# A short bfloat16 product of constants behind 38 columns of a two-block transformer kernel

## The chip, the core and the metric

The kernel runs on one core of a Trainium2 chip. The metric is the device time of one execution, in microseconds (us). The core's engines are TensorE (PE in the profile; its weight loads are listed as PEld), VectorE (DVE), ScalarE (ACT), GpSimd (POOL) and SyncE (SP). Each takes its instructions in order from a queue of its own, and they wait for one another by semaphores. The granted clock is the share of TensorE's full clock that the profile records.

## What is computed

A sequence of 256 tokens of width 1024 goes through two blocks in float32. The first has latent attention, retention, cross attention to a memory and a mixture of experts. The second is the part where the change lies:

```python
def hybrid_layer(x, p_i, ...):
    h = rmsnorm(x, g_mix)
    z = h @ w_in                       # seven parts of 1024 columns
    ...
    y_rnn = jax.nn.gelu(rnn_y) * rg_lru(rnn_x, ...)
    merged = jax.nn.sigmoid(gate_rnn) * y_rnn + jax.nn.sigmoid(gate_conv) * y_conv
    x = x + merged @ w_out
    h = rmsnorm(x, g_ffn)
    g, u = jnp.split(h @ w_gate_up, 2, axis=-1)
    x = x + (jax.nn.silu(g) * u) @ w_down
    gate = jax.nn.sigmoid(rmsnorm(x, g_ple) @ w_ple_gate)
    x = x + gate * (p_i @ w_ple)
```

The output is the root-mean-square norm of the result.

## The kernel before

Activations are kept transposed: features on the 128 partitions, the 256 tokens along the free dimension, so a vector of 1024 features is eight tiles of 128x256. A **column** is one such tile of the result of a dense layer. It is made by `dense_w` (lines 237 to 244): for each tile of 128 input features it takes a 128x128 block of weights and issues three products of 256 columns into one PSUM tile `d`. Three are needed because both sides are split into a high and a low part in a type that TensorE takes in one pass (float32r): high by high, low by high, high by low. A column of an input of 1024 features is 24 products, a column of the down projection (2816 features) 66.

The weights come from memory in chunks on SyncE's queue (line 175, tiles `w`, `r` and others). `Stream.split` makes units of 128x512 of them: ScalarE copies the unit into its high part `wh` (line 199), VectorE subtracts to get the low part `wl` (line 200). `Stream.blk` keeps up to three units split ahead. PSUM tiles `d` come from the pool `psd` with four buffers; the pool `psa` has three buffers of one bank each, for tiles called `a`.

The parts around the change, in the order of the program:

- Four heads of gates and recurrences. The recurrence of the second pair of heads is put off in small pieces (`bg`, run by `tick`), which are exponentials, squares, a root and scans on ScalarE and VectorE.
- Lines 1234 to 1238: eight columns `ps = col()` of 24 products; each is read by a gelu on ScalarE (line 1238, tile `xc`), which is ordered behind the root of the recurrences. The products of the gates before these columns read tile `xch`.
- Eight columns of gates, then the output projection with its residual, each with evictions on both engines; the second begins with a lead group of two columns (`lead`, line 253).
- Lines 1268 to 1277: 22 pairs of columns, gate and up, of 24 products each. VectorE scales the gate column (1272), ScalarE takes the silu, VectorE scales again (1274) and multiplies with the up column `pu` (1276); the result is split into `ach` and `acl`.
- Lines 1287 to 1292: eight columns of the down projection; VectorE adds the residual (1290) and both engines split the sum.
- Eight columns of the last gate and projection, and a tail with the final norm, whose statistic takes a tile `a` of `psa`.

Between the columns stand the sums of squares for the norms: four products each (line 332, tile `st`), one output column wide, with float32 operands. `keep_warm` (line 384) issues bfloat16 products of 256 columns of constants, 24 at the start and 16 in the first block.

The code is written with a framework that keeps the order of the program on each engine where nothing else decides, sets the semaphores itself, and reuses a pool's buffer once all that touched the tile before is done. `tc.issue_after(i)` orders the instructions in its block behind instruction `i` of the same engine.

Of the kernel before, what the change touches and what calls it, by code (L numbers as in the profile page):

```python
# [9 lines left out]
F32 = mybir.dt.float32  # L10
F32R = mybir.dt.float32r
I32 = mybir.dt.int32
BF16 = mybir.dt.bfloat16
# [5 lines left out]
P = 128  # L19
# [20 lines left out]
AHEAD = 3  # L40
LEAD_O = 3
LEAD_2 = 2

# [64 lines left out]
def block_kernel(tc, wst, cst_d, csa_d, sml_d, rw_d, dec_d, xt_d, pt_d, pos_d, out_d, dbg=None):  # L110
    nc = tc.nc
    V, S, TE = nc.vector, nc.scalar, nc.tensor
# [6 lines left out]
    psa = tc.alloc_tile_pool(name="psa", bufs=3, space=PSUM)  # L119
# [13 lines left out]
    cst = glob.tile([P, NCST], F32, name="cst")  # L133
# [7 lines left out]
    def G(name, i=0, n=1):  # L141
        a, _ = SML[name]
        return sml[:, a + i:a + i + n]
# [6 lines left out]
    class Stream:  # L150
# [28 lines left out]
        def split(self):  # L179

            if self.cpos >= CHUNKS[self.chunk]:
                nx = self.chunk + 1
                while nx in RAW:
                    nx += 1
                if nx >= self.limit:
                    return False
                self.tiles.pop(self.chunk, None)
                self.chunk = nx
                self.cpos = 0
            self.load(self.chunk + 1)  # L190
            w = self.tiles[self.chunk]
            n = min(UNIT, CHUNKS[self.chunk] - self.cpos)
            src = w[:, self.cpos:self.cpos + n]
            wh = self.wsp.tile([P, UNIT], F32R, name="wh")
            wl = self.wsp.tile([P, UNIT], F32R, name="wl")
            with contextlib.ExitStack() as st:
                for i in self.after:
                    st.enter_context(tc.issue_after(i.ins))
                S.activation(wh[:, :n], src, AF.Copy)  # L199
                V.tensor_sub(wl[:, :n], src, wh[:, :n].bitcast(F32))  # L200
            self.ready.append((wh, wl, n))
            self.cpos += n
            return True
# [26 lines left out]
    def split_g(h, l, x, g):  # L230
        S.mul(h, x, g)
        return V.scalar_tensor_tensor(l, x, g, h.bitcast(F32), op0=OP.mult, op1=OP.subtract)
# [5 lines left out]
    def dense_w(ps, kts, h, l):  # L238
        n, last = 0, 3 * len(kts) - 1
        for kt in kts:  # L240
            wh, wl = ws.blk(P)
            for a, b in ((wh, h), (wh, l), (wl, h)):
                TE.matmul(ps, a, b[:, kt], start=n == 0, stop=n == last)  # L243
                n += 1

    def lead(kts, h, l, n):

        pst = [ps_d() for _ in range(n)]
        for i, kt in enumerate(kts):
            for ps in pst:  # L250
                wh, wl = ws.blk(P)
                for j, (a, b) in enumerate(((wh, h), (wh, l), (wl, h))):
                    TE.matmul(ps, a, b[:, kt], start=i == 0 and j == 0, stop=i == len(kts) - 1 and j == 2)  # L253
        return pst

    def columns(n, kts, h, l, nl=0):
        pre = lead(kts, h, l, nl)
        for m in range(n):
            if m < nl:
                yield pre[m]  # L260
            else:
                ps = ps_d()
                dense_w(ps, kts, h, l)
                yield ps
# [9 lines left out]

    def ps_d():
        return psd.tile([P, T], F32, name="d")

    last_rsqrt = []
    last_sum = []
# [127 lines left out]
    for m in range(4):  # L407
        ps = ps_d()
        dense_w(ps, range(KT), xh, xl)
        if m < 3:  # L410
            split_g(ch[:, m], cl[:, m], ps, G("qn_g", m) if m < 2 else G("kvn_g"))
            S.activation(csq[:, m], ps, AF.Square)
            for tt in range(2):
                TE.matmul(cps[:, m // 2, tt:tt + 1], csq[:, m, tt * P:(tt + 1) * P], ones, start=m != 1 and tt == 0,
                          stop=m > 0, skip_group_check=True)
        else:
            S.mul(kpe, ps, G("kg_r"))
            S.activation(ksq[:, 4], ps, AF.Square)
        for kt in (2 * m, 2 * m + 1):
            sq.add(x0[:, kt])  # L420
# [10 lines left out]
    for m in range(6):  # L431
        ps = ps_d()
        dense_w(ps, range(2), ch, cl)
        S.activation(qsq[:, m], ps, AF.Square)
        for tt in range(2):
            TE.matmul(qst[:, 4 * tt:4 * tt + 4], qsq[:, m, tt * P:(tt + 1) * P], selh[:, m] if m < 4 else selr[:, m - 4],
                      start=m == 0 and tt == 0, stop=m == 5, skip_group_check=True)
        if m < 4:
            V.tensor_scalar(qn[:, m], ps, G("qg_n"), None, op0=OP.mult)
        else:  # L440
            S.mul(qr[:, m - 4], ps, G("qg_r"))
    kst = psa.tile([P, 2, 5], F32, name="a")
    for m in (4, 0, 1, 2, 3):
        if m < 4:
            ps = ps_d()
            dense_w(ps, (2,), ch, cl)
            S.activation(ksq[:, m], ps, AF.Square)
        for tt in range(2):
            TE.matmul(kst[:, tt, m:m + 1], ksq[:, m, tt * P:(tt + 1) * P], ones if m < 4 else C("selk")[:, 0:1],
                      start=True, stop=True)  # L450
# [155 lines left out]
    n = 0  # L606
    for h in range(4):
        if h >= 2:
            latent(h - 2)
        for m in (2 * h, 2 * h + 1, None):  # L610
            ps = ps_d()
# [57 lines left out]
    for m in range(KT):  # L669
        if m in (1, 4):  # L670
            latent(2 + m // 4)
        ps = next(cols)
# [60 lines left out]
    for h in range(4):  # L733
        ss = SumSq()
        cqT = ctmp.tile([P, 2, T], F32, name="cqT")
        for k2 in range(2):
            ps = next(cols)
# [7 lines left out]
        for it in range(2):  # L745
            sl = slice(it * P, (it + 1) * P)
            ps = psa.tile([P, T], F32, name="a")
# [15 lines left out]
    for m, ps in enumerate(columns(KT, range(KT), oh_, ol_, LEAD_O)):  # L763
# [7 lines left out]
        for tt in range(2):  # L771
            TE.matmul(lps[:, tt], xg[:, tt * P:(tt + 1) * P], rw[:, m], start=m == 0 and tt == 0,
                      stop=m == KT - 1, skip_group_check=True)
# [227 lines left out]
    for g in range(NGRP):  # L1001
# [12 lines left out]
        last = g == NGRP - 1  # L1014
# [22 lines left out]
        a = smp.tile([P, T], F32, name="ss_acc")  # L1037
# [54 lines left out]
    with tc.issue_after(mm.ins):  # L1092
        for m in range(3, KT):
            for tt in range(2):
                TE.matmul(sq3[:, tt:tt + 1], qs[:, m, tt * P:(tt + 1) * P], ones,  # L1095
                          start=m == 3 and tt == 0, stop=m == KT - 1, skip_group_check=True)
# [22 lines left out]
    def tick(n=1):  # L1119
        for _ in range(min(n, len(bg))):  # L1120
            bg.pop(0)()

    def col(raw=False):
        ps = ps_d()
        dense_w(ps, range(KT), *(rawx if raw else nrm))
        tick()
        return ps
# [55 lines left out]
    for h in range(4):  # L1183
# [33 lines left out]
        for dst, bias in ((ri, "br"), (ii, "bi")):  # L1217
            for m in range(2):
                ps = ps_d()
# [7 lines left out]
        if h == 0:  # L1227
            nrm = hl()
            for kt in range(KT):
                t = zt.tile([P, T], F32, name="t3")  # L1230
# [2 lines left out]
    show("xc", xc)  # L1233
    for m in range(KT):
        ps = col()
        tick(1 if m else 5)
        with tc.issue_after(roots[0].ins):
            S.activation(xc[:, m], ps, AF.Gelu_apprx_tanh)
# [13 lines left out]
    sq4 = SumSq()  # L1252
    for m, ps in enumerate(columns(KT, range(KT), mgh, mgl, LEAD_2)):
        V.tensor_add(x4[:, m], ps, x3[:, m])
# [14 lines left out]
    for f in range(FT):  # L1269
        pg = next(cols)  # L1270
        tg = ft.tile([P, T], F32, name="tg")
        V.tensor_mul(tg, pg, r4b)
        S.activation(tg, tg, AF.Silu)
        V.tensor_mul(tg, tg, r4b)
        pu = next(cols)
        V.tensor_mul(tg, pu, tg)
        split(ach[:, f], acl[:, f], tg)

# [8 lines left out]
    for m in range(KT):  # L1287
        ps = ps_d()
        dense_w(ps, range(FT), ach, acl)
        V.tensor_add(x5[:, m], ps, x4[:, m])  # L1290
        split_g(x5h[:, m], x5l[:, m], x5[:, m], G("ple_g", m))
        sq5.add(x5[:, m], last=m == KT - 1)
# [9 lines left out]
    for m in range(KT):  # L1302
        pl = ps_d()
        dense_w(pl, range(2), pth, ptl)
        ps = ps_d()
        dense_w(ps, range(KT), x5h, x5l)
        t = ft.tile([P, T], F32, name="tg")
# [19 lines left out]
    for m in range(KT):  # L1327
        V.tensor_mul(x6[:, m], x6[:, m], r6b)  # L1328
        if m % 2 == 0 or m == KT - 1:
            a = max(m - 1, 0) if m < KT - 1 else m  # L1330
# [49 lines left out]
def _blocks_w(w, cols, kts, lead=0):  # L1380

    k = w.shape[0]
    a = w.reshape(k // P, P, w.shape[1])
    parts = [a[t][:, c] for t in range(kts if lead else 0) for c in cols[:lead]]
    parts += [a[:, :, c].transpose(1, 0, 2).reshape(P, -1) for c in cols[lead:]]
    return np.concatenate(parts, 1)
# [7 lines left out]
def _cols(lo, n):  # L1394
    return [np.arange(lo + P * m, lo + P * (m + 1)) for m in range(n)]


def _pack(inp):
# [29 lines left out]
    def col(o, c):  # L1428
        return [np.arange(P) + P * c + D * o]
# [10 lines left out]
    for o in (1, 5):  # L1440
        parts.append(_blocks_w(w, [col(o, c)[0] for c in range(KT)], 8))
    parts.append(_blocks_w(g("w_out_2")[0], _cols(0, 8), 8, LEAD_2))
    w = g("w_gate_up_2")[0]
# [93 lines left out]
```

## Time and profile before

| | |
|---|---|
| median of 3 runs | 884.67 us |
| the runs | 881.99, 884.67, 886.38 us |
| the profiled execution | 884.14 us, of which the span is 882.5 us |
| mean granted TensorE clock | 0.983 |
| TensorE products, weight loads | 6508 each |
| dense products of `dense_w` over tiles `hh`, `ll` | 3624, 280 to 282 ns each |

A row of the profile gives the line of the kernel, the engine, the operation and the tiles, output before the arrow and inputs behind it, with the numbers of buffers left out. The products are pipelined: one has a duration of 280 ns, but the next starts about 117 ns after it. So a price of TensorE's time is read from the distance of the starts, not from durations. The span runs from the first to the last instruction; times of rows count from its start.

### The profile page before, as it was taken

To read this page: it belongs to the slowest core of one execution; us is meant where nothing else is said; L and a number is where in the kernel's file an instruction comes from. 1 tells how busy PE (TensorE), PEld (TensorE's weight loads), DVE (VectorE), ACT (ScalarE), POOL (GpSimd) and SP (SyncE) were. 2 spreads that over 40 slices of the span, in tenths; PEclk is the share of its full clock that TensorE was granted. 3 is DMA by queue.
4 is the path that set the end of the run, shared out by engine and by line. 5 is a ranking of instruction groups with operands and counts; after the bars stand their busy time and mean duration, and the time that the engine had idled before them with its cause. 6 is when DMAs were issued, how large, how long until landed. Compare 5 with 4: busy or idle time off the path is not lost.

```text
span 882.5 us, 16760 instructions
## 1 busy us (share of the span) xinstructions
PE 834.6 (95%) x6508; PEld 722.4 (82%) x6508; DVE 558.2 (63%) x1445; ACT 460.4 (52%) x947; POOL 3.0 (0%) x9
## 2 busy tenths in 40 slices
PE   8999999999899998699789999999999999999995
PEld 7888897999784554244349999999999999999995
DVE  6798868767663111011059959757987777766675
ACT  7696565665422111011046778777766555555563
POOL 0000000000000000000000000000000000000000
PEclk9999999999999999899989999999999999999998
DMA  8253543579769999999997546555655555553401
GB/s 326 97 209 143 192 155 113 184 296 402 302 266 410 425 426 422 423 424 423 427 423 274 202 154 215 192 179 202 208 187 192 184 179 181 182 186 136 135 16 48
DMA packets 32677, 214.90 MB, mean 244 GB/s; under 512 B 3792, under 2 KB 4688, under 8 KB 8272
## 3 DMA queue, kind: packets, MB, share of 16 engines
q1 hardware_dynamic: 31680, 212.06, 62.5%
q8 instruction: 53, 0.87, 0.4%
q0 software_dynamic: 336, 1.05, 0.3%
q10 hardware_dynamic: 576, 0.66, 0.2%
q14 instruction: 32, 0.26, 0.1%
HBM read 212.70 MB, written 1.05 MB: 242 GB/s over the span
## 4 chain that ended last, share of the span: by engine, by line
PE 49%; DMA 6%; DVE 2%; ACT 1%; issue 0%; DVEq 0%; ACTq 0%; SPq 0%
PE d L243 43%; DMA w<-wst 3%; DMA ll<-wst 2%; PE a L1021 2%; PE a L1072 1%; PE d L1058 1%; PE d L253 1%; PE st L855 1%; PE a L855 1%; ACT wh L199 0%; DVE xs L1328 0%; DVE wl L200 0%; ACT aa L1158 0%; PE a L1095 0%; DVE hs L1170 0%
## 5 line engine op out<-in xcount | busy, mean ns | idle before, releaser
L243 PE MATMUL d<-hh,wl 128*128 128x256 f32 x1208 | 340.2, 282 | 1.3 <-DVE wl L200 1.2
L243 PE MATMUL d<-hh,wh 128*128 128x256 f32 x1208 | 339.9, 282 | 1.1 <-ACT wh L199 1.1
L243 PE MATMUL d<-ll,wh 128*128 128x256 f32 x1208 | 338.4, 280 | 0.0
L199 ACT ACTIVATE wh<-w 128x512 fp32r<-128x512 f32 (+1 forms) x291 | 180.1, 627 | 135.6 <-PE d L243 103.6
L200 DVE TENSOR_TENSOR wl<-w,wh 128x512 fp32r<-128x512 f32 (+1 forms) x291 | 197.2, 685 | 60.8 <-ACT wh L199 57.7
L243 PEld LDWEIGHTS d<-hh,wl 128*128 128x128 f32 x1208 | 227.8, 189 | 2.8 <-DVE wl L200 2.3
L243 PEld LDWEIGHTS d<-ll,wh 128*128 128x128 f32 x1208 | 228.0, 189 | 1.2 <-issue 1.0
L243 PEld LDWEIGHTS d<-hh,wh 128*128 128x128 f32 x1208 | 226.9, 188 | 2.3 <-ACT wh L199 1.6
L199 ACT ACTIVATE wh<-r 128x512 fp32r<-128x512 f32 (+1 forms) x126 | 77.3, 623 | 53.4 <-PE d L243 48.8
L200 DVE TENSOR_TENSOR wl<-r,wh 128x512 fp32r<-128x512 f32 (+1 forms) x126 | 84.7, 681 | 29.0 <-ACT wh L199 27.1
L243 PE MATMUL d<-ach,wl 128*128 128x256 f32 x176 | 49.3, 280 | 0.0
L243 PE MATMUL d<-ach,wh 128*128 128x256 f32 x176 | 49.1, 279 | 0.0
L243 PE MATMUL d<-acl,wh 128*128 128x256 f32 x176 | 49.1, 279 | 0.0
L1081 DVE COPY y<-a 128x256 f32<-128x256 f32 x16 | 6.8, 424 | 60.6 <-ACT y L1080 60.6
L1038 ACT ACTIVATE ss_acc<-a,gsl 128x256 f32<-128x256 f32 x8 | 3.8, 474 | 75.6 <-DVE gsl L1028 54.2
L1058 PEld LDWEIGHTS d<-ss_sq,y 128*128 128x128 f32 x128 | 23.0, 190 | 14.9 <-ACT y L1080 6.6
L1058 PE MATMUL d<-ss_sq,y 128*128 128x256 f32 x128 | 31.6, 388 | 3.1 <-ACT y L1080 2.6
L243 PEld LDWEIGHTS d<-acl,wh 128*128 128x128 f32 x176 | 33.1, 188 | 0.0
L243 PEld LDWEIGHTS d<-ach,wl 128*128 128x128 f32 x176 | 33.0, 188 | 0.0
L243 PEld LDWEIGHTS d<-ach,wh 128*128 128x128 f32 x176 | 32.9, 187 | 0.0
L855 PEld LDWEIGHTS a<-ss_sq,xt 128*128 128x128 f32 x136 | 16.9, 191 | 15.4 <-issue 6.7
L855 PEld LDWEIGHTS st<-ss_sq,xt 128*128 128x128 f32 x120 | 14.9, 191 | 14.0 <-issue 7.5
(456 smaller groups left out, 1236.4 us busy)
## 6 DMA issues: line engine op xcount, KB each, us to landing
w<-wst SPq DMA_DIRECT2D x83, 1024.0 KB, 4.9
r<-wst SPq DMA_DIRECT2D x39, 1024.0 KB, 5.0
rx<-wst SPq DMA_DIRECT2D x28, 1024.0 KB, 17.4
ll<-wst SPq DMA_DIRECT2D x9, 1024.0 KB, 19.5
hh<-wst SPq DMA_DIRECT2D x9, 1024.0 KB, 19.5
rz<-wst SPq DMA_DIRECT2D x8, 1024.0 KB, 19.5
ck<-wst SPq DMA_DIRECT2D x5, 1024.0 KB, 19.6
cv<-wst SPq DMA_DIRECT2D x5, 1024.0 KB, 19.6
```

What stands on the lines that cost most here:

```text
L199: S.activation(wh[:, :n], src, AF.Copy)
L200: V.tensor_sub(wl[:, :n], src, wh[:, :n].bitcast(F32))
L243: TE.matmul(ps, a, b[:, kt], start=n == 0, stop=n == last)
L253: TE.matmul(ps, a, b[:, kt], start=i == 0 and j == 0, stop=i == len(kts) - 1 and j == 2)
L855: TE.matmul(ps[:, j], xt[:, tt, kt * P:(kt + 1) * P], oneh[:, tt], start=tt == 0, stop=tt == 1)
L1021: TE.matmul(pg[32 * q:32 * q + 32], xgs[:, kt, 32 * q:32 * q + 32], w[:, 512 * q:512 * q + 512], start=kt == 0, stop=kt == KT - 1)
L1038: S.activation(a, pg[:, 0:T], AF.Silu, scale=gsl[:, 4:5])
L1058: mm = ins = TE.matmul(acc[m], y[:, m % 4 * P:(m % 4 + 1) * P], sc, start=False, stop=last, skip_group_check=True)
L1072: ins = TE.matmul(py[32 * q:32 * q + 32], at[:, f, 32 * q:32 * q + 32], w[:, 512 * q:512 * q + 512], start=f == 0, stop=f == 1)
L1081: V.tensor_copy(y[:, 256:512], py[:, 256:512])
```

## The change

A function `beat(n)` is added. It issues one bfloat16 product: the first 128 columns of the constants' identity matrix, read as 256 bfloat16 values, give the 128x128 weights (the first 128) and the moving side (the first n), and the result goes into a tile `a` of `psa` that all beats share and nobody reads. `dense_w` records its last product, and the beat is ordered behind it. A beat is issued behind each of the eight gelu columns, behind each of the 22 up columns and behind each of the eight down columns, with n = 32, 64, 128, 256 by turns.

```diff
+BEATS = (32, 64, 128, 256)
...
         for kt in kts:
             wh, wl = ws.blk(P)
             for a, b in ((wh, h), (wh, l), (wl, h)):
-                TE.matmul(ps, a, b[:, kt], start=n == 0, stop=n == last)
+                last_product[:] = [TE.matmul(ps, a, b[:, kt], start=n == 0, stop=n == last)]
                 n += 1
...
+    last_product = []
+    beats = []
+
+    def beat(n):
+
+        t = cst[:, 0:128].bitcast(BF16)
+        if not beats:
+            beats.append(psa.tile([P, 512], F32, name="a"))
+        with tc.issue_after(last_product[0].ins):
+            TE.matmul(beats[0][:, 0:n], t[:, 0:P], t[:, 0:n], start=True, stop=True)
...
     for m in range(KT):
         ps = col()
+        beat(BEATS[m % 4])
         tick(1 if m else 5)
...
         pu = next(cols)
+        beat(BEATS[f % 4])
         V.tensor_mul(tg, pu, tg)
...
         dense_w(ps, range(FT), ach, acl)
+        beat(BEATS[m % 4])
         V.tensor_add(x5[:, m], ps, x4[:, m])
```

## Rows read from the trace of the kernel before

**Rows 1.** The page, first part: busy time and share of each engine.

```profile
PE 834.6 (95%) x6508; PEld 722.4 (82%) x6508; DVE 558.2 (63%) x1445; ACT 460.4 (52%) x947; POOL 3.0 (0%) x9
```

**Rows 2.** Stretches from 560 us on: length, busy (count) per engine, clock, DMA.

```profile
core 0: us, PE busy (x) PEld busy (x) DVE busy (x) ACT busy (x) POOL busy (x), PEclk, DMA share, GB/s
560.00:600.00 40.00, 39.44 (x335) 39.23 (x335) 28.14 (x55) 30.31 (x59) 0.00 (x0) 1.00 0.48 168
600.00:840.00 240.00, 239.82 (x2038) 239.65 (x2037) 179.94 (x351) 143.29 (x269) 0.54 (x1) 1.00 0.51 182
```

**Rows 3.** TensorE's waits from 580 us to 882 us.

```profile
PE a L332 <- DVE ss_sq L318: 2.0, 1, 2.0
PE st L354 <- DVE r L1325: 1.4, 1, 1.4
PE d L243 <- DVE wl L200: 0.6, 1, 0.6
PE st L354 <- DVE r L304: 0.2, 1, 0.2
```

**Rows 4.** The chain that ended last, dense phase: start, us, what.

```profile
599.17 32.55 PE d L243 x274
...
660.40 181.97 PE d L243 x1545
```

**Rows 5.** The same chain from 580 us to 600 us.

```profile
582.81 0.63 ACT wh L199
...
598.52 0.61 DVE wl L200
```

**Rows 6.** TensorE's products around 599 us, in order of time.

```profile
598.34 0.28 PE L243 MATMUL d<-ll,wh 128*128 128x256 f32 x1
599.17 0.39 PE L243 MATMUL d<-hh,wl 128*128 128x256 f32 x1 [0.56 <-DVE wl L200]
```

**Rows 7.** The chain again: last products into an `a` tile before.

```profile
462.46 0.34 PE a L1095 x4
```

**Rows 8.** Products and weight loads around a sum of squares at 654 us.

```profile
654.05 0.28 PE L243 MATMUL d<-hh,wl 128*128 128x256 f32 x1
654.17 0.50 PE L332 MATMUL st<-cst,ss_acc 128*128 128x1 f32 x4
...
654.73 0.28 PE L243 MATMUL d<-ll,wh 128*128 128x256 f32 x1
...
654.06 0.53 PEld L332 LDWEIGHTS st<-cst,ss_acc 128*128 128x128 f32 x4
654.50 0.19 PEld L243 LDWEIGHTS d<-hh,wh 128*128 128x128 f32 x1
```

**Rows 9.** Weight loads of bfloat16 products of 32 columns, first block.

```profile
262.68 0.12 PEld L826 LDWEIGHTS <-oneb 128*128 128x128 bf16 x2 [0.48 <-issue]
262.73 0.12 PEld L826 LDWEIGHTS <-ltb 128*128 128x128 bf16 x2
262.78 0.17 PEld L826 LDWEIGHTS <-oneb 128*128 128x128 bf16 x4
```

**Rows 10.** The 16 bfloat16 products of `keep_warm` and the one ahead.

```profile
260.13 0.38 PE L789 MATMUL d<-xs,cst 128*128 128x256 f32 x1
260.35 1.91 PE L384 MATMUL a<-cst 128*128 128x256 bf16 x16
...
260.14 0.10 PEld L384 LDWEIGHTS <-cst 128*128 128x128 bf16 x1
260.35 0.21 PEld L384 LDWEIGHTS <-cst 128*128 128x128 bf16 x2
```

**Rows 11.** Last gate products, and the gelus of columns 0 to 4.

```profile
L243 PE MATMUL d<-xch,wl x32: 279/280/280, 489.2 to 585.4; 128*128 128x256 f32 x32
...
595.70 0.94 ACT L1238 ACTIVATE xc<-d 128x256 f32<-128x256 f32 x3
...
L1238 ACT ACTIVATE xc<-d x1: 384/384/384, 600.7 to 600.7; 128x256 f32<-128x256 f32 x1
```

## The prediction

> **What bounds the kernel now.** I read the page first, then the stretches, the waits, the chain, and last single products.
>
> The page has TensorE busy for 95% of the span and both elementwise engines far below it [rows 1]. That is an average, so the stretches decide. All 38 new products belong to the part from the last pair of recurrences to the end. From 600 us to 840 us TensorE is busy in 239.8 of 240 us, the granted clock reads 1.00, and VectorE and ScalarE are busy for 75 and 60% [rows 2]. After 580 us the engine waits for others four times: 0.6 us for a weight split, 0.2 us for a statistic, and 2.0 and 1.4 us in the tail [rows 3]. The chain says the same: it runs through TensorE alone for 274 dense products and later for 1545 in one piece of 181.97 us, 117.8 ns each [rows 4]. In such a piece any time that a new instruction takes from TensorE is time of the kernel.
>
> The one place where TensorE isn't the bound lies before 599 us. There the chain leaves it at 582.81 and runs over ScalarE and VectorE (splits, exponentials, a root, table loads, scans, one last split) until 599.13 [rows 5]. TensorE works on beside it, issues a product at 598.34 and the next only at 599.17 [rows 6]: 0.83 us where 0.12 is usual, so 0.71 us are lost, and they end with that split, whatever TensorE did before.
>
> **The change part by part.** Nothing is removed. Recording the last product in a list is Python and adds no instruction. Each beat adds one weight load and one product to TensorE, 76 instructions in all. No DMA is issued and no step is moved past a queue.
>
> *Waits.* The new tile takes one of three banks used before by the experts and their sums; the last of those products ends at 462.8 [rows 7], over 120 us before the first beat, so its wait is met. The final statistic takes another of the three. Nobody reads a beat; what reads a column waits for that column's last product, ahead of the beat. I take nothing for all of these: the cover is that distance, and without it the columns queued behind the first beat, and the splits behind them, would wait once.
>
> *Price of one beat.* The nearest rows are the four one-column products of a sum of squares set between dense products [rows 8]. Their four loads start at 654.06 and the load behind them at 654.50: 110 ns each, although each product moves one column. From the dense product at 654.05 to the second one behind the four, at 654.73, there are 0.68 us; two spacings of 117.8 ns [rows 4] would be 0.236; so four cost 0.444, **0.111 us each**. The reason is in the same rows: a load starts when the product ahead of it starts (654.06 beside 654.05), so only one load runs ahead, and a 128x128 float32 load takes 110 ns.
>
> A beat's own load is bfloat16. Eight such loads follow one another at about 25 ns [rows 9], so it hides under the dense product ahead. But the dense load behind it can start only when the beat starts, and takes 110 ns. The run of bfloat16 products shows that one load ahead holds here too: the first starts beside the float32 product ahead (260.14 and 260.13), the second beside its own product (260.35), though the first was done at 260.24 [rows 10]. Those products are 256 wide, and 16 of them take 1.91 us; without the last one's 0.27 that is 15 spacings of 109 ns. So even the widest beat is no longer than the load that runs under it, and all four widths cost the same. I take 0.111 for each.
>
> The trace never shows a bfloat16 product directly ahead of a dense one, so the price has ends. The low one is 25 ns for 32 columns and 109 for 256 [rows 9, 10]. The high one adds the end of a product: a dense one takes 280 ns [rows 8] with starts 118 apart, so a full wait for it is 0.162, and with the load 0.273. Below nothing I don't go: the clock is already full, and TensorE idles 0.74 us in all from 560 to 840 [rows 2]. The sum-of-squares row is nearest: same place, a short product, the same load behind.
>
> By the Trainium skill (TensorE: Matmul & The Clock Gate, Back-to-back issue gap) a product costs its columns over 2.4 GHz plus 2.5 ns, never under about 25 ns. The sum by that rule would be an estimated 1.8 us, and the one-column products at 110 ns speak against it here.
>
> *How many count.* The last gate product before the eight gelu columns starts at 585.4 [rows 11]. A column is 24 products, 2.83 us, so columns 0 to 3 end near 588.3, 591.2, 594.0 and 596.8, and column 4 is cut by the stall: the first gelus run at 595.7, the fifth at 600.7. Four beats thus fall ahead of the stall and take 4 x 0.111 = 0.44 of its 0.71 us: hidden. Were that cover gone, they would cost 0.44. The other four, the 22 behind the up columns and the 8 behind the down columns lie in pieces without slack: 34 x 0.111 = **3.8 us**. The 0.2 us wait for a statistic [rows 3] stays as long as it is, because all that feeds it shifts with TensorE.
>
> The profiled execution took 884.14 (span 882.5 and 1.64 around it), so it would become 887.9. It lies 0.53 under the median, 884.67; on the median the sum is 888.5, of which I forecast **888.4**, 0.42% more. About 0.5%, 4.4 us, is what a measurement of this kernel can tell from no change, and the forecast lies just inside.
>
> **The rivals.**
>
> Width alone (14%). The dense load goes ahead of the beat as well, and only the columns cost, at 109/256 ns each but not under the 25 of rows 9: 25, 27, 55 and 109 ns. The exposed beats are 9, 9, 8 and 8 of the four widths, so 0.23 + 0.24 + 0.44 + 0.87 = 1.8 us: 886.5. For it: bfloat16 loads are short. Against it: rows 10, where a load waits for the product ahead though the one before is done. By that rule of the Trainium skill this would be the case.
>
> Width on top (13%). The dense load starts only when the beat's columns are through. Then the columns come on top of the 3.8 us: 9 x 14 + 9 x 27 + 8 x 55 + 8 x 109 ns = 1.7, together 5.5: 890.2, **slower** by 0.6%. For it: nothing shows this load beside a bfloat16 product. Against it: dense loads run under dense products everywhere. It decides as soon as a 256-wide beat costs clearly more than a 32-wide one with the load included.
>
> A drain at each change of type (6%). 34 x 0.273 = 9.3 us: 894.0. Against it: going from float32 to bfloat16 at 260.13 costs the ordinary 0.22 [rows 10]; the way back is not shown.
>
> Beats in idle time (6%). The beats are only ordered behind a product, so the program might place them in the waits, which sum to 4.2 us [rows 3], as much as 38 beats need: 884.7, not slower. Against it: nothing holds a beat once its column is issued, and the large waits lie in the tail.
>
> **How the numbers follow.** The forecast has 58%: 34 to 38 beats at 110 to 118 ns, 3.7 to 4.5 us, 888.4 to 889.2. A remaining 3% is a changed order of instructions that happens to help. The range 885.6 to 891.2 takes in the forecast, width alone and width on top with about a microsecond around them, and leaves out the drain, the idle time and some of the edges, some 20%. Faster by over 0.5%: 0.05, from the last 3% and the spread of the runs (881.99 to 886.38). Slower: the drain, most of width on top, and 17 of the forecast's 58%, since its upper end crosses 889.1: 0.34. The rest, 0.61, is within 0.5%.
>
> **What would show it.** Right: behind each beat the dense load starts with the beat and the dense product about 110 ns later, for all four widths; the dense piece after 660 us is about 22 + 8 beats or 3.3 us longer; the stall before 599 us shrinks by some 0.4 us; the clock stays at 1.00. Wrong: a cost that grows with the width, a gap ahead of the first dense product behind a beat, a column's reader that waits for the beat, or a stall at 599 us that keeps its length.

## The result, and the profile after

The changed kernel takes 888.15 us (median of 20 runs, 885.85 to 890.41). The kernel before takes 883.23 (20 runs, 875.90 to 886.38). The ratio is 1.0055, with a 95% interval from 1.0041 to 1.0070: slower by 4.9 us, between 3.6 and 6.2. The forecast was 888.4, as a rise of 3.7 on the median of three runs known then, 884.67; that median lay 1.4 above the one of 20 runs.

The two profiled executions seem to say less: spans of 882.5 before and 884.1 after, 1.6 apart. But the part ahead of the change differs from run to run. A mark that all kernels share is the last group of four products of the sums behind the experts; it is the last thing ahead of the pieces in which the change lies. TensorE in order of time, kernel after:

```profile
458.51 0.50 PE L1107 MATMUL a<-cst,qs 128*128 128x1 f32 x4
```

In the execution before, the same group, which [rows 7] show as a step of the chain, starts at 462.30 in the order of time. So the part in front was 3.8 us shorter in the execution after, though the change does nothing there; in three repeats of the kernel before the mark lies at 459.5 to 460.8. The part from the mark to the end of the span, called the **late part** from here on, is 425.6 us against 420.2.

The late part ends with a tail that differs from run to run too. A second mark leaves it out: the group of four products behind the last column of the down projection, which comes right behind the last beat. Both marks, kernel before:

```profile
462.30 0.50 PE L1095 MATMUL a<-cst,qs 128*128 128x1 f32 x4
...
842.20 0.50 PE L332 MATMUL st<-cst,ss_acc 128*128 128x1 f32 x4
```

The second mark, kernel after:

```profile
842.68 0.50 PE L344 MATMUL st<-cst,ss_acc 128*128 128x1 f32 x4
```

The part between the marks, called the **dense part**, is 379.90 us before and 384.17 after. In the three repeats it is 379.92, 379.91 and 379.90. So against the mean of these four, 379.91, which agree within 0.02 us, the beats cost **4.26 us** in one execution of the changed kernel.

The stretches after answer to [rows 2] (length, busy time and count of each engine, clock, DMA):

```profile
core 0: us, PE busy (x) PEld busy (x) DVE busy (x) ACT busy (x) POOL busy (x), PEclk, DMA share, GB/s
560.00:600.00 40.00, 39.95 (x339) 39.49 (x338) 28.24 (x54) 30.08 (x58) 0.00 (x0) 1.00 0.47 170
600.00:840.00 240.00, 239.82 (x2035) 238.27 (x2035) 176.28 (x344) 140.06 (x263) 0.54 (x1) 1.00 0.50 178
```

TensorE is as full as before and the clock is still 1.00. In the first stretch 0.05 us of idle time are left of 0.56. The stall, which lay ahead of 599 us, is at 595 us here and much shorter: the products on its two sides start 0.32 us apart (595.06 and 595.38). The list of TensorE's waits from 580 us on says it too. It has the other three waits of [rows 3] with the same length, and the one for the weight split is missing:

```profile
PE a L344 <- DVE ss_sq L330: 2.0, 1, 2.0
PE st L366 <- DVE r L1340: 1.4, 1, 1.4
PE st L366 <- DVE r L316: 0.2, 1, 0.2
```

Now single beats. First one of 32 columns and one of 256, TensorE's products in order of time (start, duration):

```profile
596.51 0.28 PE L244 MATMUL d<-hh,wl 128*128 128x256 f32 x1
596.63 0.19 PE L288 MATMUL a<-cst 128*128 128x32 bf16 x1
596.67 0.36 PE L244 MATMUL d<-hh,wh 128*128 128x256 f32 x1
596.87 0.28 PE L244 MATMUL d<-ll,wh 128*128 128x256 f32 x1
...
593.28 0.28 PE L244 MATMUL d<-hh,wl 128*128 128x256 f32 x1
593.40 0.28 PE L288 MATMUL a<-cst 128*128 128x256 bf16 x1
593.44 0.36 PE L244 MATMUL d<-hh,wh 128*128 128x256 f32 x1
593.64 0.28 PE L244 MATMUL d<-ll,wh 128*128 128x256 f32 x1
```

From the last dense product ahead of the beat to the second one behind it there are 0.36 us in both, 0.125 more than two spacings of 117.8 ns. All 37 beats that have a dense product behind them, of all four widths, show 0.357 to 0.364 us, in the mean 0.362: a price of 0.126. The first dense product behind a beat is recorded 0.04 us after it, whatever the width; the delay shows at the second, 0.20 us further on. The loads around the 256 wide one:

```profile
593.17 0.19 PEld L244 LDWEIGHTS d<-hh,wl 128*128 128x128 f32 x1
593.40 0.10 PEld L288 LDWEIGHTS <-cst 128*128 128x128 bf16 x1
593.40 0.20 PEld L244 LDWEIGHTS d<-hh,wh 128*128 128x128 f32 x1
593.53 0.19 PEld L244 LDWEIGHTS d<-ll,wh 128*128 128x128 f32 x1
```

The dense load starts with the beat, at 593.40, as forecast. The beat's own load does not start beside the dense product ahead, at 593.28, but at 593.40 too.

The chain no longer has one piece of 1545 products as in [rows 4], but pieces of two columns with a beat between them. Every fourth begins at the same place of the pattern:

```profile
658.17 5.75 PE d L244 x48
...
681.29 5.75 PE d L244 x48
```

These 23.12 us hold 192 dense products and one beat of each width; less 192 x 0.1178 there are 0.50 left, 0.125 for each beat. No instruction is shown to wait for a beat.

### The profile page after: what moved, and what is told of

It is laid out like the page before. It is cut to its first block, busy times and chain, and to the rows that moved or that the text cites. A ratio compares the mean times of both kernels' runs of the same rounds, so it can differ in the third digit from the quotient of the medians.

```text
span 884.1 us, 16837 instructions
## 1 busy us (share of the span) xinstructions
PE 839.0 (95%) x6546; PEld 723.9 (82%) x6546; DVE 558.1 (63%) x1445; ACT 460.2 (52%) x947; POOL 3.0 (0%) x9
## 4 chain that ended last, share of the span: by engine, by line
PE 71%; DMA 16%; DVE 6%; ACT 5%; issue 2%; DVEq 0%; ACTq 0%; SPq 0%
PE d L244 55%; DMA rx<-wst 5%; PE a L1033 2%; DMA rz<-wst 2%; DMA r<-wst 2%; DMA ck<-wst 2%; DMA cv<-wst 2%; DMA w<-wst 2%; ACT wh L200 2%; DVE wl L201 1%; PE d L254 1%; PE a L1084 1%; PE a L867 1%; PE d L1070 1%; PE a L740 1%
```

## The experiments

Two theories stood against each other. By the load theory a beat costs the load of the dense product behind it, and its own columns count only beyond that. By the slot theory each inserted product costs a slot of its own; a third has the columns on top of the load. All kernels below ran once, with a profile, so they are compared by single distances, by the dense part and by the late part, not by the time, which carries the spread of the front part.

**The kernel before, three times more.**

> The kernel before once more, for its pace. Pace theory: the 1545 dense products behind the last statistic ahead of the gate and up columns run at one pace, drawn when they start: 117.8 ns, as in the profile of before, with a time near 883 us, or 113.4 ns with a time near 876 us (1545 x 4.4 ns = 6.8 us). Rival: the pace is always 117.8 there, and the spread of the runs of before comes from elsewhere (the experts' stage, the start).

> The kernel before once more, to catch an execution whose long pieces run at the fast pace. Pace theory: wherever the time is under 881 us, a long piece behind 460 us has a spacing of about 113.4 ns; otherwise all have 117.8. Rival: low times come from the part ahead of 460 us alone.

> As the run before it: pace theory, a time under 881 us goes with a long piece at 113.4 ns behind 460 us; rival, it goes with a shorter part ahead of 460 us.

The times were 882.99, 882.52 and 883.57 us. The late parts are 421.1, 421.4 and 421.1 us: 421.2 within 0.2. In all three the long piece ran at 117.8 ns (181.97 and 181.96 us for 1545 products, as in [rows 4]). No execution came out under 881 us, so what makes the rare low times of the kernel before was not seen. What differs most is the part in front, as the rival has it: in the twelve profiles of this case, of all kernels, the first mark lies between 458.5 and 464.5 us. The profile of before, with a late part of 420.2, is the odd one: its last dense products, 173 from 851.61 on, ran at 113.4 ns instead of 117.8 (0.8 us less), and its last two transposes took 0.42 us instead of 0.62 to 0.68. Against the repeats the changed kernel costs 4.4 us in the late part, 4.26 of them in the dense part.

**Two beats in place of one.**

```diff
-BEATS = (32, 64, 128, 256)
+BEATS = (32, 32, 32, 32)
...
         with tc.issue_after(last_product[0].ins):
-            TE.matmul(beats[0][:, 0:n], t[:, 0:P], t[:, 0:n], start=True, stop=True)
+            for _ in range(2):
+                TE.matmul(beats[0][:, 0:n], t[:, 0:P], t[:, 0:n], start=True, stop=True)
```

> Every beat is two bfloat16 products of 32 columns, one behind the other. From the changed kernel: the last dense product ahead of a beat and the second one behind it are 0.36 us apart, 0.125 more than two spacings. Load theory (a beat costs the load of the dense product behind it, which starts with the last beat): the second product adds only about 25 ns, so 0.385 us apart, and some 34 x 0.025 = 0.9 us more than the changed kernel. Slot theory (each inserted product costs a slot of its own): 0.485 us apart, 34 x 0.125 = 4.3 us more.

TensorE in order of time, kernel with two beats:

```profile
681.50 0.28 PE L244 MATMUL d<-hh,wl 128*128 128x256 f32 x1
681.62 0.21 PE L289 MATMUL a<-cst 128*128 128x32 bf16 x2
681.68 0.36 PE L244 MATMUL d<-hh,wh 128*128 128x256 f32 x1
681.88 0.28 PE L244 MATMUL d<-ll,wh 128*128 128x256 f32 x1
```

The distance is 0.38 here and 0.387 in the mean of 28 places: the second product adds 25 ns. The dense part is 385.00 us, 0.8 more than with single beats. The slot theory, which wanted 0.485 and 4.3, falls.

**Beats of 512 columns.**

```diff
-            TE.matmul(beats[0][:, 0:n], t[:, 0:P], t[:, 0:n], start=True, stop=True)
+            TE.matmul(beats[0].rearrange("p (a b) -> p a b", a=4), t[:, 0:P], t[:, None, 0:P].to_broadcast([P, 4, P]), start=True, stop=True)
```

> Every beat has 512 columns (the 128 constants four times over). Load theory: the columns, 2 x 109 = 218 ns, now outlast the load of 110 ns, so the price is about 0.22 to 0.23 and the distance from the last dense product ahead to the second behind about 0.46 us; some 34 x 0.1 = 3.4 us more than the changed kernel. Slot theory: 0.36 as for all other widths. Columns on top of the load: 0.24 + 0.11 + 0.22 = 0.57 us. Pace: if a beat sets the slow pace of the dense products because they then wait for loads, the pace behind a 512 wide beat, whose load is early, may be the fast one of 113.4 ns; if any interruption sets the slow one it is 117.8.

Kernel with beats of 512 columns, products in order of time:

```profile
668.31 0.28 PE L244 MATMUL d<-hh,wl 128*128 128x256 f32 x1
668.43 0.39 PE L288 MATMUL a<-cst 128*128 128x512 bf16 x1
668.47 0.47 PE L244 MATMUL d<-hh,wh 128*128 128x256 f32 x1
668.77 0.28 PE L244 MATMUL d<-ll,wh 128*128 128x256 f32 x1
```

0.46 us, 0.467 in the mean of 27: a price of 0.231. That is 218 ns of columns and 13 ns more. The load, which runs under the columns from 668.43 on, no longer shows. The dense part is 387.93 us, 8.0 more than before, and 3.8 more than with the changed kernel, where 3.4 were expected. Of this 0.1 comes from the first four beats, which cost 0.92 us here and outgrow the stall. Columns on top of the load would have been 0.57 and fall too. The pace behind the beat was 117.8, so a wide beat doesn't bring the fast one.

**Beats of one float32 column.**

```diff
-            TE.matmul(beats[0][:, 0:n], t[:, 0:P], t[:, 0:n], start=True, stop=True)
+            TE.matmul(beats[0][:, 0:1], ident, ones, start=True, stop=True)
```

> Every beat is a float32 product of one column with the same weights, as in a sum of squares. If the 0.125 of a bfloat16 beat is the 0.111 of the sums plus some 14 ns that are due to the type or to its own load starting late, the distance from the last dense product ahead to the second behind falls to 0.346 us. If every single interruption costs 0.125 (and four in a row share it), it stays at 0.36 us.

Neither value came: the distance is 0.46 us. The rows of this kernel say why:

```profile
668.42 0.28 PE L244 MATMUL d<-hh,wl 128*128 128x256 f32 x1
668.54 0.28 PE L288 MATMUL a<-cst 128*128 128x1 f32 x2
668.68 0.37 PE L244 MATMUL d<-hh,wh 128*128 128x256 f32 x1
668.88 0.28 PE L244 MATMUL d<-ll,wh 128*128 128x256 f32 x1
...
668.42 0.31 PEld L288 LDWEIGHTS a<-cst 128*128 128x128 f32 x2
668.65 0.19 PEld L244 LDWEIGHTS d<-hh,wh 128*128 128x128 f32 x1
```

One float32 product of the program is two products with two loads on the chip: the trace has 76 more products than before for 38 beats. The price of 0.225 is 2 x 0.112, so per load it is the 0.111 of the sums of squares. The dense part is 387.59 us, 7.7 more than before, as 34 x 0.225 = 7.65 would have it. The four products of [rows 8] were two of the program. The first load of a beat starts beside the dense product ahead here (668.42), and the 14 ns by which a bfloat16 beat is dearer are not there.

**Beats in the type of the dense products.**

```diff
-    def beat(n):
-
-        t = cst[:, 0:128].bitcast(BF16)
+    def beat(s):
+
...
-            TE.matmul(beats[0][:, 0:n], t[:, 0:P], t[:, 0:n], start=True, stop=True)
+            TE.matmul(beats[0][:, 0:T], s[:, 0, 0:P], s[:, 0], start=True, stop=True)
```

The calls pass `nrm[0]`, `x4h` and `ach`.

> Every beat is a float32r product of 256 columns, in type and size like the dense ones, from tiles written long before. Load theory: its own load runs under the dense product ahead, so a beat costs one slot of the dense pace, 0.118 us: the last dense product ahead and the second behind are 0.353 us apart. The 0.36 (0.125) of the bfloat16 beats is then due to their own load, which starts only when the dense product ahead has streamed. If any product that interrupts a column costs 0.125, it stays at 0.36.

Loads and products of this kernel:

```profile
689.99 0.28 PE L244 MATMUL d<-hh,wl 128*128 128x256 f32 x1
690.10 0.28 PE L287 MATMUL a<-hh 128*128 128x256 f32 x1
690.22 0.28 PE L244 MATMUL d<-hh,wh 128*128 128x256 f32 x1
690.34 0.28 PE L244 MATMUL d<-ll,wh 128*128 128x256 f32 x1
...
689.99 0.19 PEld L287 LDWEIGHTS a<-hh 128*128 128x128 f32 x1
690.11 0.19 PEld L244 LDWEIGHTS d<-hh,wh 128*128 128x128 f32 x1
```

0.35 us: the beat takes one slot of the dense pace and nothing else. Its load starts at 689.99 with the product ahead. The dense part is 383.88 us, 4.0 more than before, which is 34 x 0.117, and 0.29 less than with bfloat16 beats. So a bfloat16 beat, whose own load starts late, is some 10 ns dearer than a float32r beat and some 14 ns dearer than a load of [rows 8]. In these runs the extra goes with the late start; that the late start makes it was not tried apart from the type. Why a bfloat16 load behind a float32r product starts 0.12 us later than a load of the same type, though [rows 10] show one that starts beside a float32 product, stays open.

**Only the first beats.** One kernel keeps the beats of the first four gelu columns, the other those of all eight.

```diff
         ps = col()
-        beat(BEATS[m % 4])
+        if m < 4:
+            beat(BEATS[m % 4])
...
         pu = next(cols)
-        beat(BEATS[f % 4])
...
         dense_w(ps, range(FT), ach, acl)
-        beat(BEATS[m % 4])
```

> Only the four beats behind the first four gelu columns are left. If the wait ahead of the last weight split takes them up, the part from the last sum of squares of the experts (the last four products of that line) to the end of the span stays at the 421.1 to 421.4 us of the three repeats of the kernel before. If they count like the others it is 421.7, and the wait keeps its 0.83 us.

> Only the eight beats behind the gelu columns are left. With the first four hidden and four at 0.125 us each, the part from the last sum of squares of the experts to the end of the span is about 421.2 + 0.5 = 421.7 us; if all eight count, 422.2.

Kernel with four beats, around the stall:

```profile
599.61 0.28 PE L244 MATMUL d<-ll,wh 128*128 128x256 f32 x1
599.93 0.38 PE L244 MATMUL d<-hh,wl 128*128 128x256 f32 x1
```

The gap is 0.32 us instead of 0.83: the four beats took 0.51 of it. From the first mark to the second product behind the stall there are 137.09 us (463.06 to 600.15); in the profile of before, the first repeat and the changed kernel there are 137.1 too, within 0.01. The four beats are hidden. The late part of 421.4 us says the same less finely, since the tail is in it. The second mark, with four beats and then with eight:

```profile
842.96 0.50 PE L344 MATMUL st<-cst,ss_acc 128*128 128x1 f32 x4
```

```profile
844.88 0.50 PE L344 MATMUL st<-cst,ss_acc 128*128 128x1 f32 x4
```

With four beats the dense part is 379.90 us (842.96 less 463.06), as without any: they cost nothing. With eight, where the first mark is at 464.51, it is 380.37: 0.47 more, which is four beats at 0.12 and not eight, for which 1.0 would be due. The late part with eight beats, 420.6 us, doesn't fit the 421.7 that were expected, because the last dense products ran at 113.3 ns and the last transposes took 0.42 us, as in the profile of before; both lie behind the last beat.

**Another order of the three products.** A try at the pace, without beats:

```diff
-            for a, b in ((wh, h), (wh, l), (wl, h)):
+            for a, b in ((wh, h), (wl, h), (wh, l)):
```

> The kernel before with the second and third product of each triple exchanged (high by high, high by low, low by high becomes: weights high, low, high). No beats. The question is whether the slow pace hangs on the order of loads: if it does, the spacing in the long pieces differs from 117.8 ns (113.4 would be 20 us less in all); if it is drawn at each wait whatever the order, the long pieces show 117.8 or 113.4 as before and the time stays near 883 us.

886.16 us, and 181.97 us for the 1545 products: the pace doesn't hang on this order. The late part is 422.6 us, 1.4 longer than the repeats; a wait of 0.6 us for a sum of squares is new. No version came out ahead of the kernel before.

## Why the prediction was right, step by step

*What bounds it.* Right. TensorE's time is the kernel's time behind 600 us, and what the beats take there arrives at the end.

*The price.* The mechanism was right and the term too small: 0.125 us instead of 0.111, the same for all four widths. The load of the dense product behind, 110 ns, starts with the beat and covers up to 256 columns; at 512 the columns come out. The step that failed is "it hides under the dense product ahead", said of the beat's own load from [rows 9]; [rows 10], where such a load starts beside a float32 product, seemed to bear it out. Here the load starts 0.12 us after the product ahead, together with the beat, and with it goes the extra of 14 ns. It is not the number of products: a second beat behind the first costs 25 ns, as the loads of [rows 9] do. The reading of [rows 8] as four products was wrong in name, since they are two of the program, but each load has its 111 ns, so the value held. One sign came otherwise than forecast: the dense product behind a beat was to start about 110 ns after it, and is recorded 0.04 us after it; the delay shows at the second dense product.

*How many count.* Right: 34. The first four lie ahead of the stall, shorten it by 0.51 us and don't move its end. 34 x 0.125 = 4.25, against 4.26 measured in the dense part, 4.4 in the late part over the repeats and 4.9 (3.6 to 6.2) over the runs. The dense piece behind 660 us with its 30 beats grew by 3.8 us, where 3.3 were forecast.

*The rivals.* Width alone (1.8 us) falls with the equal distances of all widths. Width on top wanted 0.46 us for 256 columns, and the drain 0.51 for all; both fall with 0.36 us, and width on top with the beats of 512 columns too. Idle time: the beats stand where the program has them, and the two large waits of the tail are unchanged.

The forecast of 0.42% said "just inside" half a per cent. The measured 0.55% lies just outside, with an interval on both sides of it; the missing 14 ns on 34 beats, 0.5 us, are part of this, and the rest is within the interval. That 888.4 came so near to 888.15 is in part luck: the median it was built on was 1.4 us too high and the rise 1.2 too low, and the two errors nearly cancel. The range for the rise itself, 3.7 to 4.5 us, takes in the 4.26, but as 34 beats at 0.125 and not at the 110 to 118 ns that it was built from.

By the rule of the Trainium skill (TensorE: Matmul & The Clock Gate, Back-to-back issue gap) the beats would have cost an estimated 1.8 us. That section of the Trainium skill gives the rule for a product by itself, and says that in a stream of loads and products both set the spacing and that the rule counts too little for few columns, which the prediction left out. The runs agree with that limit where each product brings a new 128x128 float32 load: there 32 columns cost as much as 256. Where the weights behind are bfloat16 the rule's 25 ns hold, as the second beat shows.

## What to carry to other kernels

In a stream like this one, where each product brings a new 128x128 load of 110 ns, a short product costs the load of the product behind it, not its own columns. Count the loads that can't run under a long enough product, not the columns, and put small bfloat16 products next to each other rather than one by one: the second of two cost 25 ns. Compare single executions between two marks that both share, ahead of the change and behind it, or the spread of the parts around it hides an effect of half a per cent.

## What the runs showed besides

The dense products have two paces, 117.8 ns and about 113.4 ns, at a clock of 1.00 in both. In the late parts a pace changed only where the products were interrupted. In the profile of before, the last 173 products took the fast one from 851.61 on, behind a longer spacing of 0.19 us, and so did the same products with eight beats. In the three repeats and in the changed kernel they ran at the slow one:

```profile
846.66 23.41 PE d L243 x198
```

This is the first repeat; the profile of before has 22.65 us for the same 198. These products lie behind the last beat of every kernel, so both paces came with beats and without. Twice a fast stretch right behind the stall met a beat: nine products from 595.60 on in the changed kernel and nine from 601.61 on in the one with eight beats, at 113.4 ns both. Both times 117.8 followed. Whether beats end a fast stretch, two cases don't show. What sets the pace was not found.
